# Small weights loaded half by half between x's tile pairs, and multiplied with the first pair before the second pair is transposed

## The chip, the core and the metric

The kernel runs on one core of a Trainium2 chip. The metric is the device time of one execution in microseconds (us). The core has five engines that run side by side, each through its own instructions in order: TensorE (PE in the profile, its weight loads PEld), VectorE (DVE), ScalarE (ACT), GpSimd (POOL) and SyncE (SP), which here only issues DMA transfers. Matrix products land in PSUM, and everything else is kept in SBUF.

## The reference, cut to what matters

One encoder layer over 512 tokens of width 1024: an RMS norm, one wide input projection, sparse attention over keys that an indexer picks (group A), latent attention (group B), gates, and one output projection with a residual. The change lies wholly in the first lines: the norm, and the two narrow columns of the projection.

```python
xn = rms_norm(h, norm_gain[l])          # (512, 1024)
proj = xn @ w_in[l]                     # (1024, D_IN)
(q_a, k_a, v_a, g_a, q_i, k_i, w_i,
 c_q, c_kv, k_rope, g_b) = jnp.split(proj, offsets, axis=-1)
...
k_i = jnp.concatenate([rope(k_i[..., :IDX_ROPE_DIM], pos), k_i[..., IDX_ROPE_DIM:]], axis=-1)
o_a = indexer_sparse_attention(q_a, k_a, v_a, q_i, k_i, w_i, pos)
```

The "small weights" are 104 of w_in's columns: 32 for `k_rope`, and 72 for `k_i` and `w_i`. `q_i` is the first wide projection (512 columns).

## The kernel before, in words

Every matrix product is made of three, because each operand is kept as a high part (rounded to the type that TensorE reads) and a low part (what the rounding left): high times high, high times low, low times high. `mm3` (L180) issues these three. So every operand costs two steps before TensorE can use it: a copy or scaling that makes the high part, nearly always on ACT, and a subtraction that makes the low part, on DVE or POOL.

The start of the program runs as follows. The token dimension is cut in four tiles of 128 (t = 0 to 3), and tiles 0 and 1 are the first pair (`xin` 0, half 0), tiles 2 and 3 the second (`xin` 1, half 1). Per tile: a DMA loads it (L198). ACT sums the squares of its first 512 columns and DVE those of the other 512 (L343, L344), DVE adds the two sums (L345), POOL raises the sum to the power -0.5 (`rsqrt`, L216), and DVE scales the tile with that (L350), in one instruction of 1024 columns, for tile 3 in two of 512. Then TensorE transposes the tile in eight pieces of 128 columns (`x_turn`, L130) into PSUM, eight k-pieces per pair. When both tiles of a pair are there, ACT makes `xh` from PSUM (L370) and DVE makes `xl` (L373), 16 instructions each over the whole start.

The small weights `smw` come by four DMAs (two halves of four k-pieces, each in a transfer of 32 and one of 72 columns), ACT casts each half to `swh` (L204), and POOL subtracts for `swl` (L205). `small_step(hf, k)` multiplies k-piece k of one pair (half hf of the tokens) with them: 3 products of 256 columns into the bank `sm_acc`.

The wide weights come in chunks of one k-piece: a DMA into `wst` (three buffers, L263), a cast on ACT to `wh` (L267), a subtraction to `wl` (L270) on POOL, for every fourth chunk of `q_i` on DVE. A DMA into a `wst` buffer waits until the subtraction that reads the buffer's former chunk is done. So the subtractions set the pace of the loads.

TensorE's order is the order of the code. Before: the transposes of all four tiles, then `small_step(0, 0..7)`, then `small_step(1, k)` in turns with steps of `q_i` for tiles 1 to 3. The order on the other engines comes from a scheduler that works on an estimate of times, within the order that `after` (L221) forces by hand.

Later, `use_small` transposes the small result on TensorE, ACT copies it to `sm` (L431), and a row of DVE instructions (L438 to L442, then L410, L413 and L509 for the first tile of `q_i`) leads to the transposes of that tile (`turn` in `use_qi`), which TensorE has in its order among the wide products.

Of the kernel before, what the change touches and what calls it, by code (L numbers as in the profile page):

```python
# [16 lines left out]
D = 1024  # L17
# [67 lines left out]
def layer(ctx: ExitStack, tc: tile.TileContext, x, norm_gain, w_in, a_q_norm, a_k_norm, b_q_latent,  # L85
# [11 lines left out]
    def sb(tag, shape, dt=F32, name=None):  # L97
        return P.tile(list(shape), dt, name=name or tag, tag=tag, bufs=BUFS[tag])
# [8 lines left out]
    def psum(tag):  # L107
        return PS.tile([128, 512], F32, name=tag, tag=tag, bufs=BANKS[tag])

    def f32(ap):  # L110
        return ap.bitcast(F32)
# [39 lines left out]
    def run(g):  # L151
        for _ in g:
            tick()

    def take(g, n):
        for _ in range(n):
            if next(g, None) is None:
                return
            yield 1
# [34 lines left out]
    wst = sb("qk8", (128, 8, 104), name="smw")  # L194
    wv = w_in.rearrange("(k p) c -> p k c", p=128)
    SWH, SWL = sb("V", (128, 8, 104), F32R, "swh"), sb("V", (128, 8, 104), F32R, "swl")
    for t in range(NT):
        nc.sync.dma_start(xin[t // 2][:, t % 2], xv[:, t])  # L198
        if t == NT - 1:
            for a in range(0, 8, 4):  # L200
                ks = slice(a, a + 4)
                nc.sync.dma_start(wst[:, ks, 0:32], wv[:, ks, 3272:3304])
                nc.sync.dma_start(wst[:, ks, 32:104], wv[:, ks, 2560:2632])
                nc.scalar.copy(SWH[:, ks], wst[:, ks])  # L204
                nc.gpsimd.tensor_tensor(SWL[:, ks], wst[:, ks], f32(SWH[:, ks]), op=OP.subtract)  # L205
        if t == 1:
            nc.sync.dma_start(ident, cst[:, 768:896])
            nc.sync.dma_start(grow[0:8], norm_gain.rearrange("(k p) -> k p", p=128))
            nc.sync.dma_start(grow[8:11], b_q_latent.rearrange("(k p) -> k p", p=128))
            nc.sync.dma_start(grow[11:13], b_kv_latent.rearrange("(k p) -> k p", p=128))  # L210

    nhalf = P.tile([128, 8], F32, name="nhalf")
    nc.gpsimd.memset(nhalf, -0.5)
# [97 lines left out]
    def stream(jobs, group=2, banks=("mm",), skew=True):  # L311

        order, start = [], 0
        for i, (nk, _, _) in enumerate(jobs):
            s = start if skew else start - start % nk
            order += [(s + k, i, k) for k in range(nk)]
            start += nk / group
        acc = {}
        for _, i, k in sorted(order):
            nk, step, use = jobs[i]  # L320
            if k == 0:
                acc[i] = psum(banks[i % len(banks)])
            step(acc[i], k)
            if k == nk - 1:
                use(acc.pop(i))
            yield 1
# [12 lines left out]
    for t in range(NT):  # L339
        xt = xin[t // 2][:, t % 2]  # L340
        r = small(4)
        sq = tmp(), tmp()
        nc.scalar.activation(sq[0], xt[:, 0:512], AF.Square, scale=D ** -0.5, accum_out=r[:, 0:1])  # L343
        nc.vector.tensor_tensor_reduce(sq[1], xt[:, 512:], xt[:, 512:], 1.0 / D, EPS, OP.mult, OP.add, r[:, 1:2])  # L344
        nc.vector.tensor_tensor(r[:, 2:3], r[:, 0:1], r[:, 1:2], op=OP.add)  # L345
        rsqrt(r[:, 3:4], r[:, 2:3])
        w = D // 2 if t == NT - 1 else D
        for a in range(0, D, w):
            xs = xt[:, a:a + w]
            nc.vector.tensor_scalar(xs, xs, r[:, 3:4], None, op0=OP.mult)  # L350
    gp = psum("pv")
    transpose(gp[:, :13], grow[:13], ident[:13, :13])
    nc.scalar.copy(gains, gp[:, :13])


    xb = {}

    def x_turn(t):
        hf = t // 2
        if t % 2 == 0:  # L360
            xb[hf] = [psum(b) for b in (("tr", "tr", "sc", "sc"), ("mm", "mm", "mm", "tr"))[hf]]
        for k in range(8):
            c = (k % 2) * 256 + (t % 2) * 128
            transpose(xb[hf][k // 2][:, c:c + 128], xin[hf][:, t % 2, k * 128:k * 128 + 128], ident)
        parts = lambda k: [xb[hf][k // 2][:, (k % 2) * 256:(k % 2) * 256 + 256]] + [
            f(k)[:, hf * 256:hf * 256 + 256] for f in (xh, xl)]
        for b in range(0, 8 if t % 2 else 0, 2):
            for k in (b, b + 1):
                p, h, l = parts(k)
                nc.scalar.activation(h, p, AF.Copy, scale=gains[:, k:k + 1])  # L370
            for k in (b, b + 1):
                p, h, l = parts(k)
                nc.vector.scalar_tensor_tensor(l, p, gains[:, k:k + 1], f32(h), op0=OP.mult, op1=OP.subtract)  # L373
# [98 lines left out]
    def lat_kv(_, a):  # L472
        latent(a, 11, ckv, ckvs, "pt2")

    for t in range(NT):
        x_turn(t)
    sm_acc = psum("pv")

    def small_step(hf, k):
        c = slice(hf * 256, hf * 256 + 256)  # L480
        mm3(sm_acc[:104, c], SWH[:, k], SWL[:, k], xh(k)[:, c], xl(k)[:, c], k == 0, k == 7)

    for k in range(8):
        small_step(0, k)
    qi_ = stream(tok_jobs("q_i", 8, xh, xl, 512, [1, 2, 3], lambda t, a: use_qi(t, a)), 3, skew=True)
    for k in range(8):
        small_step(1, k)
        run(take(qi_, 1))
        if k == 2:
            nc.sync.dma_start(cs32, cst[:, 512:768])  # L490
    nc.sync.dma_start(wide, cst[:, 896:1408])
# [474 lines left out]
```

## Time and profile before

| | us |
|---|---|
| median of 3 runs | 347.33 (346.73 to 347.7) |
| the profiled execution | 345.63 |
| its span in the trace | 343.8 |
| around the span (345.63 - 343.8) | 1.83 |
| TensorE busy | 326.7 (95% of the span) |
| DVE busy | 265.5 (77%) |
| ACT busy | 219.6 (64%) |
| POOL busy | 182.2 (53%) |

The trace is one execution; engines are rows of instructions with a start and a duration. Where an instruction found its engine idle, a bracket says how long the engine sat idle and whose work ended the wait. Start-up is the time in which TensorE is not yet busy without breaks, here the first 13.3 us. TensorE's granted clock is at its full 2.4 GHz throughout.

### The profile page before, as it was taken

How to read it: one execution, taken by the hardware profiler on the slowest of the kernel's cores; microseconds unless marked ns; L12 is line 12 of the kernel's file. 1: busy time of each engine (PE TensorE's matmuls, PEld its weight loads, DVE VectorE, ACT ScalarE, POOL GpSimd, SP SyncE). 2: the span in 40 equal slices, each digit the busy share in tenths (PEclk: the TensorE clock that was granted, in tenths of full speed). 3: DMA queues.
4: the chain of work that ended last, by engine and by line, in shares of the span. 5: the costliest groups of instructions: out<-in, count | busy, mean ns of one | idle time of the engine just before them, and what ended most of it. 6: DMA issues, size and time to landing. Idle time of an engine off the chain costs nothing.

```text
span 343.8 us, 5465 instructions
## 1 busy us (share of the span) xinstructions
PE 326.7 (95%) x1688; PEld 271.9 (79%) x1688; DVE 265.5 (77%) x634; ACT 219.6 (64%) x536; POOL 182.2 (53%) x193
## 2 busy tenths in 40 slices
PE   2999899999899999999999999999999999999995
PEld 2887787888688788788888788888888788788884
DVE  4925787759999797877779987679898776877466
ACT  4934558574757776878876898434526988878210
POOL 1745462166697998315623469519924635457100
PEclk9999999999999999999999999999999999999999
DMA  7753344124032433103320055515697324410006
GB/s 267 196 151 98 84 132 126 29 94 122 2 99 71 113 92 102 54 2 92 92 64 0 1 128 159 144 24 141 170 212 216 126 79 137 120 66 0 2 0 244
DMA packets 28806, 34.83 MB, mean 101 GB/s; under 512 B 5341, under 2 KB 16874, under 8 KB 28778
## 3 DMA queue, kind: packets, MB, share of 16 engines
q1 hardware_dynamic: 28202, 33.57, 34.7%
q10 hardware_dynamic: 576, 0.92, 0.7%
q8 instruction: 13, 0.21, 0.3%
q14 instruction: 15, 0.12, 0.1%
HBM read 27.14 MB, written 2.10 MB: 85 GB/s over the span
## 4 chain that ended last, share of the span: by engine, by line
PE 49%; DVE 17%; POOL 11%; DMA 8%; issue 6%; ACT 6%; SPq 1%; POOLq 0%; DVEq 0%; ACTq 0%
PE mm L126 28%; PE sc L126 7%; DMA wst<-in_w_in 7%; PE pv L126 6%; PE tr L130 5%; POOL wl L270 4%; POOL sml L216 4%; DVE acc L555 2%; DVE ob L923 2%; DVE m L554 2%; PE mm L130 2%; DVE z L694 2%; ACT wh L267 2%; ACT z L696 1%; DVE wl L270 1%
## 5 line engine op out<-in xcount | busy, mean ns | idle before, releaser
L270 POOL TENSOR_TENSOR wl<-wst,wh 128x512 fp32r<-128x512 f32 (+2 forms) x79 | 98.3, 1253 | 59.3 <-ACT wh L267 47.9
L267 ACT CAST wh<-wst 128x512 fp32r<-128x512 f32 (+2 forms) x89 | 50.9, 586 | 30.2 <-DMA wst<-in_w_in 22.0
L126 PE MATMUL mm<-wh,xh 128*128 128x512 f32 x120 | 50.2, 419 | 0.0
L126 PE MATMUL mm<-wl,xh 128*128 128x512 f32 x120 | 47.6, 397 | 0.2 <-POOL wl L270 0.2
L126 PE MATMUL mm<-wh,xl 128*128 128x512 f32 x120 | 47.4, 395 | 0.0
L216 POOL TENSOR_TENSOR sml<-sml,nhalf 128x4 f32<-128x4 f32 (+2 forms) x28 | 32.0, 1149 | 25.9 <-ACT sml L825 14.8
L696 ACT ACTIVATE z<-z,sml 128x256 f32<-128x256 f32 (+2 forms) x64 | 35.9, 561 | 11.1 <-DVE sml L694 10.0
L713 POOL TENSOR_SCALAR z<-z,sml 128x512 f32<-128x512 f32 (+2 forms) x32 | 18.2, 570 | 41.6 <-DVE sml L709 31.4
L126 PE MATMUL mm<-xh,wh 128*128 128x512 f32 x80 | 33.3, 417 | 0.0
L126 PE MATMUL mm<-xl,wh 128*128 128x512 f32 x80 | 31.7, 396 | 0.0
L126 PE MATMUL mm<-xh,wl 128*128 128x512 f32 x80 | 31.6, 395 | 0.0
L126 PEld LDWEIGHTS mm<-wh,xl 128*128 128x128 f32 x120 | 22.6, 188 | 5.3
L554 DVE MAX8 m<-acc 128x8 f32<-128x512 f32 (+2 forms) x48 | 26.3, 549 | 0.0
L555 DVE MATCH_REPLACE8 acc<-m,acc 128x512 f32<-128x512 f32 (+2 forms) x48 | 25.9, 540 | 0.0
L126 PEld LDWEIGHTS mm<-wl,xh 128*128 128x128 f32 x120 | 22.8, 190 | 3.5 <-POOL wl L270 0.5
L126 PEld LDWEIGHTS mm<-wh,xh 128*128 128x128 f32 x120 | 22.7, 189 | 3.0
L694 DVE CUSTOM_DVE_ANT_0 z<-sc,wide,nqb 128x512 f32<-128x512 f32 (+3 forms) x32 | 17.4, 543 | 6.4 <-PE sc L126 6.2
L416 DVE TENSOR_TENSOR pl<-tr,ph 128x512 fp32r<-128x512 f32 (+1 forms) x32 | 17.6, 551 | 5.9 <-ACT ph L416 5.6
L416 ACT CAST ph<-tr 128x512 fp32r<-128x512 f32 (+1 forms) x32 | 15.2, 474 | 8.0 <-PE tr L130 7.6
L126 PE MATMUL sc<-kl,bhl 96*128 96x512 f32 (+3 forms) x96 | 20.2, 322 | 0.0
L126 PEld LDWEIGHTS sc<-kl,bhl 96*128 96x128 f32 x96 | 16.6, 189 | 3.2 <-DVE bhl L794 0.3
L923 DVE TENSOR_TENSOR ob<-mm,ob 128x512 f32<-128x512 f32 (+1 forms) x25 | 16.5, 667 | 2.9 <-PE mm L126 2.6
(214 smaller groups left out, 884.6 us busy)
## 6 DMA issues: line engine op xcount, KB each, us to landing
wst<-in_w_in SPq DMA_DIRECT2D x48, 256.0 KB, 2.7
wst<-in_w_out SPq DMA_DIRECT2D x16, 256.0 KB, 2.9
xin<-in_x SPq DMA_DIRECT2D x4, 512.0 KB, 4.1
k_a<-tmp SPq DMA_DIRECT2D x16, 128.0 KB, 3.5
ob<-in_x SPq DMA_DIRECT2D x8, 256.0 KB, 4.5
wst<-in_w_in SPq DMA_DIRECT2D x8, 192.0 KB, 2.6
wst<-in_w_uq SPq DMA_DIRECT2D x6, 192.0 KB, 2.3
wst<-in_w_in SPq DMA_DIRECT2D x8, 128.0 KB, 2.1
```

The costliest lines, as they stand in the source:

```text
L126: nc.tensor.matmul(o, l, r, start=start, stop=stop)
L130: nc.tensor.transpose(o, i, idn)
L216: nc.gpsimd.tensor_tensor(dst, src, nhalf[:, :src.shape[-1]], op=OP.pow)
L267: copies.append(nc.scalar.copy(h, st))
L270: i = E(eng).tensor_tensor(l, st, f32(h), op=OP.subtract)
L416: return nc.scalar.copy(h, p), nc.vector.tensor_tensor(l, p, f32(h), op=OP.subtract)
L554: nc.vector.max(m, masks[t])
L555: dve[0] = nc.vector.match_replace(masks[t], m, masks[t], -3e38).ins
L694: m = nc.vector.tensor_tensor_reduce(z, sc[:, :n], mask(t), nq(h, t), 3e38, OP.add, OP.min, r[:, i:i + 1])
L696: e = nc.scalar.activation(z, z, AF.Exp, bias=r[:, i:i + 1], scale=-1.0, accum_out=r[:, 2 + i:3 + i])
L713: nc.gpsimd.tensor_scalar(z, z, w, 0.0, op0=OP.mult, op1=OP.add)
L923: nc.vector.tensor_tensor(o, p[:, :n], o, op=OP.add)
```

## The change

The four small constant loads (`ident` and three gains) go from SP's DMA queue to ACT's, ahead of ACT's work. On SP's queue the first half of the small weights comes after tiles 0 and 1 and the second half after tiles 2 and 3. TensorE transposes tiles 0 and 1, does `small_step(0, 0..3)`, transposes tiles 2 and 3, and goes on with `small_step(0, 4..7)`. The second half of tile 3 is scaled on ACT instead of DVE. Three orders are forced by hand: the sum of squares of tile 3 on ACT behind the `xh` of the first pair's k-piece 3, the cast of the second half of the small weights behind the scaling of tile 3's second half, and the casts of the first three `q_i` chunks behind the cast of the small weights and each behind two more `xh`.

```diff
+    nc.scalar.dma_start(ident, cst[:, 768:896])
+    nc.scalar.dma_start(grow[0:8], norm_gain.rearrange("(k p) -> k p", p=128))
+    nc.scalar.dma_start(grow[8:11], b_q_latent.rearrange("(k p) -> k p", p=128))
+    nc.scalar.dma_start(grow[11:13], b_kv_latent.rearrange("(k p) -> k p", p=128))
     for t in range(NT):
         nc.sync.dma_start(xin[t // 2][:, t % 2], xv[:, t])
-        if t == NT - 1:
-            for a in range(0, 8, 4):
-                ks = slice(a, a + 4)
-                nc.sync.dma_start(wst[:, ks, 0:32], wv[:, ks, 3272:3304])
-                nc.sync.dma_start(wst[:, ks, 32:104], wv[:, ks, 2560:2632])
-                nc.scalar.copy(SWH[:, ks], wst[:, ks])
-                nc.gpsimd.tensor_tensor(SWL[:, ks], wst[:, ks], f32(SWH[:, ks]), op=OP.subtract)
-        if t == 1:
-            nc.sync.dma_start(ident, cst[:, 768:896])
...
+        if t % 2:
+            ks = slice(t // 2 * 4, t // 2 * 4 + 4)
+            nc.sync.dma_start(wst[:, ks, 0:32], wv[:, ks, 3272:3304])
+            nc.sync.dma_start(wst[:, ks, 32:104], wv[:, ks, 2560:2632])
+            swc = nc.scalar.copy(SWH[:, ks], wst[:, ks])
+            nc.gpsimd.tensor_tensor(SWL[:, ks], wst[:, ks], f32(SWH[:, ks]), op=OP.subtract)
...
             xs = xt[:, a:a + w]
-            nc.vector.tensor_scalar(xs, xs, r[:, 3:4], None, op0=OP.mult)
+            if a:
+                xsc = nc.scalar.activation(xs, xs, AF.Copy, scale=r[:, 3:4])
+            else:
+                nc.vector.tensor_scalar(xs, xs, r[:, 3:4], None, op0=OP.mult)
...
-                nc.scalar.activation(h, p, AF.Copy, scale=gains[:, k:k + 1])
+                e = nc.scalar.activation(h, p, AF.Copy, scale=gains[:, k:k + 1])
+                xev[hf, k] = e
+                if (hf, k) == (0, 3):
+                    after(sqa, e)
...
-    for t in range(NT):
-        x_turn(t)
-    sm_acc = psum("pv")
...
+    x_turn(0)
+    x_turn(1)
+    sm_acc = psum("pv")
     for k in range(8):
+        if k == 4:
+            x_turn(2)
+            x_turn(3)
         small_step(0, k)
+    after(swc, xsc)
     qi_ = stream(tok_jobs("q_i", 8, xh, xl, 512, [1, 2, 3], lambda t, a: use_qi(t, a)), 3, skew=True)
     for k in range(8):
         small_step(1, k)
         run(take(qi_, 1))
+        if k == 0:
+            for i, c in enumerate(copies[:3]):
+                after(c, swc)
+                after(c, xev[1, 2 * i + 1])
```

TensorE, start of the program, as a difference (`xin_63` is the first pair, `xin_64` the second; `pv<-xh,swh` and its like are the small products, of which a third use `xl` and a third `swl`):

```order
 L130 MATMUL tr<-ident,xin_63 128x128 x4
 L130 MATMUL sc<-ident,xin_63 128x128 x4
-L130 MATMUL mm<-ident,xin_64 128x128 x6
-L130 MATMUL tr<-ident,xin_64 128x128 x2
-L130 MATMUL mm<-ident,xin_64 128x128 x6
-L130 MATMUL tr<-ident,xin_64 128x128 x2
 L126 MATMUL pv<-xh_89,swh 104x256
 L126 MATMUL pv<-xl_91,swh 104x256
```

The 16 transposes of the second pair now stand behind the first 12 small products, and the other 12 small products behind those transposes.

DVE from the second tile's scaling to the last scaling, before (`ISA` with `xin` is the sum of squares, `ISA sml` its read-out, `TENSOR_SCALAR` the scaling, `SCALAR_TENSOR_TENSOR` makes `xl`):

```order
L344 ISA tmp,sml<-xin_64 128x512
L344 ISA sml 128x1
L350 TENSOR_SCALAR xin_63<-xin_63,sml 128x1024
L345 TENSOR_TENSOR sml<-sml 128x1
L344 ISA tmp,sml<-xin_64 128x512
L344 ISA sml 128x1
L350 TENSOR_SCALAR xin_64<-xin_64,sml 128x1024
L345 TENSOR_TENSOR sml<-sml 128x1
L373 SCALAR_TENSOR_TENSOR xl_91<-tr,gains,xh_89 128x256 x2
L350 TENSOR_SCALAR xin_64<-xin_64,sml 128x512 x2
L373 SCALAR_TENSOR_TENSOR xl_91<-tr,gains,xh_89 128x256 x2
```

The same place on DVE now:

```order
L352 TENSOR_SCALAR xin_63<-xin_63,sml 128x1024
L343 ISA tmp,sml<-xin_64 128x512
L343 ISA sml 128x1
L344 TENSOR_TENSOR sml<-sml 128x1
L352 TENSOR_SCALAR xin_64<-xin_64,sml 128x1024
L343 ISA tmp,sml<-xin_64 128x512
L343 ISA sml 128x1
L378 SCALAR_TENSOR_TENSOR xl_91<-tr,gains,xh_89 128x256 x4
L344 TENSOR_TENSOR sml<-sml 128x1
L378 SCALAR_TENSOR_TENSOR xl_92<-sc,gains,xh_90 128x256 x4
L352 TENSOR_SCALAR xin_64<-xin_64,sml 128x512
```

Each tile's scaling now stands directly behind that tile's sum, and the last scaling stands behind all eight `xl` of the first pair instead of behind two.

POOL at the same place now (`sml<-sml,nhalf` is the power -0.5 of one tile; before, all four stood in a row, and both `swl` behind them):

```order
L215 ISA
L215 TENSOR_TENSOR sml<-sml,nhalf 128x1 x2
L209 TENSOR_TENSOR swl<-smw,swh 128x416
L215 TENSOR_TENSOR sml<-sml,nhalf 128x1 x2
L209 TENSOR_TENSOR swl<-smw,swh 128x416
L269 TENSOR_TENSOR wl<-wst,wh 128x512 x6
```

The first `swl` has moved between the powers of tiles 1 and 2.

ACT from the sum of squares of tile 2 on, now (`xh` of the second pair is written from `mm` and the last `tr`, `wh` are the chunks of `q_i`; before, the first `wh` stood ahead of the second pair's first `xh`):

```order
L342 ACTIVATE tmp,sml<-xin_64 128x512
L372 ACTIVATE xh_89<-tr,gains 128x256 x4
L342 ACTIVATE tmp,sml<-xin_64 128x512
L372 ACTIVATE xh_90<-sc,gains 128x256 x4
L350 ACTIVATE xin_64<-xin_64,sml 128x512
L208 CAST swh<-smw 128x416
L372 ACTIVATE xh_89<-mm,gains 128x256 x2
L266 CAST wh<-wst 128x512
L372 ACTIVATE xh_89<-mm,gains 128x256 x2
L266 CAST wh<-wst 128x512
```

The first two `wh` now each stand behind two `xh` of the second pair. Behind this place the rows of all engines are the same as before, but for the `wst` buffers: chunk 5 of `q_i` now takes the buffer that chunk 2 leaves, where before it took that of chunk 3.

## Rows read from the trace of the kernel before

**Rows 1.** Stretches: us, busy (x instructions) of PE, PEld, DVE, ACT, POOL; clock, DMA.

```profile
0.00:13.33 13.33, 6.17 (x33) 5.44 (x34) 8.08 (x21) 8.03 (x21) 3.90 (x11) 1.00 0.90 285
13.33:34.13 20.80, 20.59 (x115) 17.06 (x113) 10.34 (x24) 11.04 (x26) 12.39 (x12) 1.00 0.41 109
```

**Rows 2.** TensorE's waits, whole program: who waited for whom, us, times, longest.

```profile
PE sc L126 <- DVE vb L642: 2.0, 3, 1.4
PE tr L130 <- DVE tmp L509: 0.9, 1, 0.9
PE tr L126 <- DVE acc L546: 0.8, 1, 0.8
...
PE tr L130 <- DVE kil L416: 0.3, 1, 0.3
```

**Rows 3.** Timeline, TensorE: start, duration, operation, count, [idle before, releaser].

```profile
12.94 0.44 PE L130 MATMUL mm<-ident,xin 128*128 128x128 f32 x2 [0.55 <-DVE xin L350]
...
13.35 0.36 PE L126 MATMUL pv<-xh,swh 128*104 128x256 f32 x1
...
16.61 0.40 PE L126 MATMUL mm<-wh,xh 128*128 128x512 f32 x1
...
19.32 0.50 PE L126 MATMUL mm<-wl,xh 128*128 128x512 f32 x1 [0.21 <-POOL wl L270]
...
27.97 0.52 PE L130 MATMUL tr<-ident,tmp 104*128 104x104 f32 x4
...
35.07 0.63 PE L130 MATMUL tr<-ident,tmp 128*128 128x128 f32 x4 [0.94 <-DVE tmp L509]
```

**Rows 4.** Timeline, DVE, start-up.

```profile
7.13 0.69 DVE L344 CUSTOM_DVE_ANT_0 tmp<-xin 128x512 f32<-128x512 f32 x1 [0.26 <-DMA xin<-in_x]
...
7.75 0.75 DVE L350 TENSOR_SCALAR xin<-xin,sml 128x1024 f32<-128x1024 f32 x1
8.41 0.15 DVE L345 TENSOR_TENSOR sml<-sml 128x1 f32<-128x1 f32 x1
...
11.20 1.68 DVE L350 TENSOR_SCALAR xin<-xin,sml 128x512 f32<-128x512 f32 x2
...
13.60 1.64 DVE L373 SCALAR_TENSOR_TENSOR xl<-sc,gains,xh 128x256 fp32r<-128x256 f32 x4
```

**Rows 5.** Timeline, POOL, start-up.

```profile
6.95 0.56 POOL L216 TENSOR_TENSOR sml<-sml,nhalf 128x1 f32<-128x1 f32 x1 [1.19 <-DVE sml L345]
...
11.24 1.36 POOL L205 TENSOR_TENSOR swl<-smw,swh 128x416 fp32r<-128x416 f32 x1 [0.34 <-ACT swh L204]
13.51 1.09 POOL L205 TENSOR_TENSOR swl<-smw,swh 128x416 fp32r<-128x416 f32 x1 [0.90 <-ACT swh L204]
```

**Rows 6.** Timelines: DVE's second half of tile 3's scaling alone, from a narrower window.

```profile
11.60 1.29 DVE L350 TENSOR_SCALAR xin<-xin,sml 128x512 f32<-128x512 f32 x1
```

**Rows 7.** Timelines of DVE and POOL: three subtractions of the wide weights.

```profile
19.33 0.69 DVE L270 TENSOR_TENSOR wl<-wst,wh 128x512 fp32r<-128x512 f32 x1 [0.91 <-ACT wh L267]
...
25.86 1.30 POOL L270 TENSOR_TENSOR wl<-wst,wh 128x512 fp32r<-128x512 f32 x1 [1.14 <-ACT wh L267]
...
26.44 1.26 DVE L270 TENSOR_TENSOR wl<-wst,wh 128x512 fp32r<-128x512 f32 x1 [6.42 <-ACT wh L267]
```

**Rows 8.** Timeline, ACT.

```profile
9.55 1.19 ACT L370 ACTIVATE xh<-tr,gains 128x256 fp32r<-128x256 f32 x3
10.62 0.54 ACT L204 CAST swh<-smw 128x416 fp32r<-128x416 f32 x1
...
13.27 0.67 ACT L267 CAST wh<-wst 128x512 fp32r<-128x512 f32 x1
...
30.22 0.50 ACT L431 COPY sm<-tr 128x416 f32<-128x416 f32 x1
```

**Rows 9.** Timeline, SP: start and duration of the first two issues.

```profile
0.73 0.86 SPq L198 DMA_DIRECT2D xin<-in_x  x2
```

**Rows 10.** DMA issues to 30 us: KB each, median us from issue to landing.

```profile
smw<-in_w_in SPq DMA_DIRECT2D x2, 144.0 KB, 4.5
```

More of the change, by code (lines that the diff above doesn't have):

```diff
@@ L196, in layer @@
     SWH, SWL = sb("V", (128, 8, 104), F32R, "swh"), sb("V", (128, 8, 104), F32R, "swl")
+    nc.scalar.dma_start(ident, cst[:, 768:896])
+    nc.scalar.dma_start(grow[0:8], norm_gain.rearrange("(k p) -> k p", p=128))
+    nc.scalar.dma_start(grow[8:11], b_q_latent.rearrange("(k p) -> k p", p=128))
+    nc.scalar.dma_start(grow[11:13], b_kv_latent.rearrange("(k p) -> k p", p=128))
     for t in range(NT):
         nc.sync.dma_start(xin[t // 2][:, t % 2], xv[:, t])
-        if t == NT - 1:
-            for a in range(0, 8, 4):
-                ks = slice(a, a + 4)
-                nc.sync.dma_start(wst[:, ks, 0:32], wv[:, ks, 3272:3304])
-                nc.sync.dma_start(wst[:, ks, 32:104], wv[:, ks, 2560:2632])
-                nc.scalar.copy(SWH[:, ks], wst[:, ks])
-                nc.gpsimd.tensor_tensor(SWL[:, ks], wst[:, ks], f32(SWH[:, ks]), op=OP.subtract)
-        if t == 1:
-            nc.sync.dma_start(ident, cst[:, 768:896])
-            nc.sync.dma_start(grow[0:8], norm_gain.rearrange("(k p) -> k p", p=128))
-            nc.sync.dma_start(grow[8:11], b_q_latent.rearrange("(k p) -> k p", p=128))
-            nc.sync.dma_start(grow[11:13], b_kv_latent.rearrange("(k p) -> k p", p=128))
+        if t % 2:
[4 more added lines that the diff above has]
+            nc.gpsimd.tensor_tensor(SWL[:, ks], wst[:, ks], f32(SWH[:, ks]), op=OP.subtract)
     nhalf = P.tile([128, 8], F32, name="nhalf")
@@ L342, in layer @@
         sq = tmp(), tmp()
-        nc.scalar.activation(sq[0], xt[:, 0:512], AF.Square, scale=D ** -0.5, accum_out=r[:, 0:1])
+        sqa = nc.scalar.activation(sq[0], xt[:, 0:512], AF.Square, scale=D ** -0.5, accum_out=r[:, 0:1])
         nc.vector.tensor_tensor_reduce(sq[1], xt[:, 512:], xt[:, 512:], 1.0 / D, EPS, OP.mult, OP.add, r[:, 1:2])
@@ L353, in layer @@
     nc.scalar.copy(gains, gp[:, :13])
-    xb = {}
+    xb, xev = {}, {}
     def x_turn(t):
```

## The prediction

> **What bounds the kernel now.** I read the share of busy time first: TensorE is at 95% of the span, so the time is its work plus its idle time. The table of stretches says where that idle time is: of the first 13.33 us TensorE works 6.17, so 7.16 us are idle, and in the next 20.80 us it works 20.59 [rows 1]. From then on its largest waits are 2.0, 0.9, 0.8 and 0.3 us, all for DVE [rows 2]. So start-up is the one place with something to win, and a shift of TensorE there goes through to the end, unless one of those later waits takes it up.
>
> Then I read who sets start-up. DVE's rows from 7.13 to 13.60 stand end to end [rows 4]: it does one job after the other for four tiles, and TensorE's transposes of the last piece wait 0.55 us for a scaling on DVE [rows 3]. The small products then run from 13.35 without a break, and the first product of `q_i` starts at 16.61 [rows 3]. The only wait behind it up to 34.13 (35.07 less the 0.94 us of idle time before it) is at 19.32, for the third `wl` from POOL [rows 3]. So the order of work on DVE decides when the second pair is transposed, and POOL's subtractions decide when `q_i` gets going. Both are touched.
>
> **The change part by part.**
>
> What it aims at is easy to price: 12 of the small products (27 stand between 13.35 and 16.61, so 0.12 us each, 1.45 us in all [rows 3]) go into idle time. That is worth up to 1.45 us if the second pair is transposed as early as before. It is not, by the following walk, and DVE is its first half.
>
> Step 1, tile 1's scaling. POOL ends the power for tile 1 at 6.95 + 0.56 = 7.51 [rows 5]. Before, POOL then had nothing to do but the next power; now the first `swl` is next. Is its input there? SP is free behind two issues at 0.73 + 0.86 = 1.59 [rows 9], the second small transfer is issued about 0.4 later, at 2.0, lands 4.5 later [rows 10], at 6.5, and the cast takes 0.54 [rows 8]: 7.05, so yes, with half a microsecond to spare. Then POOL goes from one instruction into the next at 7.51, while DVE's scaling of tile 1 must first hear of it. What happens when the two meet is in the trace: the second half of tile 3's scaling took 1.29 us [rows 6], where the pair of halves, less this, leaves some 0.48 for the first [rows 4], and it ended at 12.89, 0.29 behind the `swl` that ran on POOL from 11.24 to 12.60 [rows 5]. A subtraction of wide weights on DVE took 1.26 us beside one on POOL that ran until 27.16, and 0.69 alone [rows 7]. So a DVE instruction that reads SBUF in this way stands still until POOL's is through. Here `swl` lasts 1.09 [rows 5], to 8.60, and the scaling, of twice the columns, ends 2 x 0.29 behind it: 9.18. Without that it would end at 7.55 + 0.75 = 8.30.
>
> The Trainium skill has the rule for this ("SBUF — State Buffer", section "Who interferes with whom"): DVE and GpSimd share one pair of SBUF ports, which whoever comes first holds for its whole instruction. It speaks against putting `swl` between two scalings, and the trace agrees with the 1.29 us against 0.48. The page also counts DVE instructions with two SBUF inputs; by that the sum of squares would be held too, and a late `swl` would cost no less than an early one: the sum is the same.
>
> Step 2, tile 2. DVE's order now is sum, add, scaling with nothing between, where before it did the next tile's sum while POOL took the power. From 9.18: the sum starts 0.08 ahead of the end and lasts 0.70 with its read-out, the add 0.15 [rows 4], to 9.95; 0.08 later POOL's power, 0.56 [rows 5], to 10.59; the scaling 0.75 [rows 4], to 11.40. So 0.7 us of DVE's time go into waiting for POOL.
>
> Step 3, to the last scaling. Sum of tile 3 to 12.02; four `xl` (1.64 for four, 0.40 from start to start [rows 4]) to 13.62; the add to 13.72; four more `xl` to 15.32; then the half of tile 3's scaling that stays on DVE, 0.48: it ends at T = 15.80. Before, both halves were done at 12.89. The half that ACT takes saves DVE 0.4 to 0.5 us and is not late: the power of tile 3 ends some 0.65 behind the add, at 14.4, and ACT needs one 0.6 us instruction. I set it at nothing.
>
> Step 4, from T to `q_i`. Two transposes, 0.44 [rows 3], and 0.05 to get there: 16.29. Two `xh` at 0.36 each (1.19 for three, with overlap [rows 8]): 17.01. Only then the first `wh`, 0.67 [rows 8], since the change puts the casts behind two `xh` each: 17.68. POOL then needs 1.30 for each `wl` [rows 7], three of them with 0.05 in front: 21.63. So the product that started at 19.32 [rows 3] starts at about 21.68, 2.36 later. TensorE's own way is as long: eight transposes at 0.22 (1.76), 12 small products (1.45), three more (0.36), then two steps of about 1.05 and one product: 15.85 + 1.76 + 1.45 + 0.36 + 2.10 + 0.23 = 21.75. The later chunks each follow the subtraction that frees their buffer and have room at this pace.
>
> Step 5, what is given back. The 0.94 us wait at 35.07 [rows 3] ends a chain of DVE work that starts with ACT's copy of the small result at 30.22 [rows 8]. TensorE had its transposes ready at 27.97 + 0.52 = 28.49 [rows 3], 1.73 earlier. With TensorE 2.36 later they end at 30.85, so the chain moves by only 0.66, and ends at 35.73, while TensorE arrives at 34.13 + 2.36 = 36.49. The wait is gone, and 2.36 - 0.94 = 1.42 us remain. The later waits [rows 2] hang on DVE instructions that follow these transposes, so they move along and give nothing back.
>
> Step 6, the four constant loads on ACT's queue. They take SP's issue time off tiles 2 and 3 and put about as much (some 1.4 us) on ACT ahead of its first input, which is idle there. Nothing.
>
> Sum: 345.63 + 1.42 = 347.05 for the profiled execution. The median of the runs is 347.33, 1.70 above that execution, so in runs it is 348.75; I say 348.7 (+0.4%). A measurement can tell about 0.3%, here 1.04 us, from no change.
>
> **Bounds.** The lower end of T is DVE's work without the stop: scaling to 8.30, tile 2's scaling to 10.52, T = 14.92, which leaves 0.54 us. The upper end is a late transfer: past 8.3 each microsecond is one on T.
>
> **The rivals.**
>
> *The port is free* (0.18): `swl` falls beside nothing, or the meeting costs less on 1024 columns than on 512. T = 14.92, and +0.54: 347.9, within 0.3%. Against it stand the two meetings [rows 6, 7].
>
> *The small transfer is late* (0.10): it now runs behind two x tiles and ahead of two. If it lands at 9.5 instead of 6.5, the cast is done at 10.04, `swl` at 11.2, and the power for tile 2, which stands behind it on POOL, at 11.8 instead of 10.59: +1.2 on top, 349.9. Its landing took 4.5 us with x tiles ahead of it too [rows 10], which speaks against so long a delay.
>
> *The loss is given back later* (0.14): the 2.0, 0.8 and 0.3 us of later waits [rows 2] are for DVE; if DVE has room by then, TensorE's delay shrinks by about as much as these waits hold, to between 0 and 0.5: 347.3 to 347.8.
>
> *Faster* (0.08): the second pair is not delayed, and the 12 products do go into idle time. The place is the last half scaling on DVE, and the point is T = 15.80 - 1.42 = 14.38: before it the change gains. At the 12.89 of before it would gain 1.49: 345.8. For it speaks that TensorE idles for 7.16 us ahead of 13.33 [rows 1]; against it, that DVE's rows alone, with no stop by POOL, already add up to 14.92.
>
> That the products don't go ahead is no rival: the order has them there. They will wait for the `xl` of their piece, from 12.4 to 13.6.
>
> **How the numbers follow.** The main case has 0.50, the rivals 0.18, 0.10, 0.14 and 0.08. Within the main case T may be off by half a microsecond, and about a fifth of it falls under 1.04 us. Slower by over 0.3%: 0.40 + 0.10 = 0.50; within 0.3%: 0.10 + 0.18 + 0.14 = 0.42; faster: 0.08. The range leaves out the faster case and the outer ends of the others: from 347.2, just under the case where all is given back, to 350.0, the late transfer.
>
> **What the profile of the changed kernel would show.** Step 1: tile 1's scaling takes 1.3 to 1.7 us beside a POOL `swl`; 0.75 would be the free port. Step 2: DVE idle for 0.6 to 0.7 us ahead of tile 2's scaling. Step 3: the first transposes of the second pair's last tile start near 15.8. Step 4: the first `wh` near 17, the third `wl` done near 21.6, TensorE waiting for it or just not. Step 5: no wait ahead of the transposes at 35.07, which now start near 36.5. The forecast is wrong if those transposes start before 35.6, or if TensorE's idle time behind them is smaller than before by a microsecond.

## The result, and the profile after

| | before | changed |
|---|---|---|
| median of 20 runs, us | 345.92 (344.65 to 347.7) | 347.95 (346.76 to 350.14) |
| ratio, 95% interval | | 1.0057 (1.004 to 1.0074) |
| the profiled execution, us | 345.63 | 348.55 |
| its span, us | 343.8 | 346.7 |
| TensorE busy, us | 326.7 | 328.8 (95%) |

The change makes the kernel 0.6% slower, about 2 us. The forecast was 1.42 us.

First the stretches of the changed kernel (us, busy and instructions of PE, PEld, DVE, ACT, POOL; clock, DMA), which answer to [rows 1]:

```profile
0.00:13.33 13.33, 4.91 (x20) 4.11 (x21) 6.93 (x17) 7.07 (x18) 3.03 (x10) 1.00 0.89 284
13.33:34.13 20.80, 20.64 (x115) 17.64 (x114) 8.96 (x21) 11.97 (x27) 11.31 (x11) 1.00 0.36 96
```

TensorE worked 6.17 us ahead of 13.33 before and works 4.91 now: of the 12 small products that were to fill the idle time, only three start in it. TensorE's waits (who for whom, us, times, longest), which answer to [rows 2], say for what it waits:

```profile
PE sc L126 <- DVE vb L654: 2.0, 3, 1.4
PE pv L126 <- DVE xl L378: 1.1, 1, 1.1
...
PE sc L126 <- DVE bhl L806: 0.3, 1, 0.3
PE tr L130 <- DVE tmp L521: 0.3, 1, 0.3
```

The small products wait 1.1 us for the first `xl`. The wait ahead of the first turn of `q_i` (`tr` for `tmp`) fell from 0.9 to 0.3, so 0.65 was given back there. The 2.0 for `vb` is as before, and 0.3 for `bhl` is new. Now TensorE in order (start, duration, operation, [idle before, releaser]), which answers to [rows 3]:

```profile
11.16 0.56 PE L126 MATMUL pv<-xh,swh 128*104 128x256 f32 x1
12.82 0.54 PE L126 MATMUL pv<-xl,swh 128*104 128x256 f32 x1 [1.10 <-DVE xl L378]
13.16 0.41 PE L126 MATMUL pv<-xh,swl 128*104 128x256 f32 x1
13.37 0.41 PE L126 MATMUL pv<-xh,swh 128*104 128x256 f32 x1
...
15.29 1.38 PE L130 MATMUL mm<-ident,xin 128*128 128x128 f32 x6
...
16.73 0.82 PE L130 MATMUL mm<-ident,xin 128*128 128x128 f32 x6
...
19.37 0.39 PE L126 MATMUL mm<-wh,xh 128*128 128x512 f32 x1
...
22.41 0.50 PE L126 MATMUL mm<-wl,xh 128*128 128x512 f32 x1
...
31.07 0.52 PE L130 MATMUL tr<-ident,tmp 104*128 104x104 f32 x4
...
37.52 0.63 PE L130 MATMUL tr<-ident,tmp 128*128 128x128 f32 x4 [0.29 <-DVE tmp L521]
```

The small products start 0.21 apart (13.16, 13.37), where the 27 of before started 0.12 apart. They hold the transposes of tile 2 until 15.29, and those of tile 3 follow at 16.73. The first product of `q_i` moved from 16.61 to 19.37, the product with the third `wl` from 19.32 to 22.41 (+3.09), and the first turn of `q_i` from 35.07 to 37.52 (+2.45). Behind that, each row of TensorE stands 2.4 us later than before up to 139, and 2.9 from 142, behind the wait for `bhl`. Nothing is given back later.

The pace of 0.21 is that of TensorE's lower clock. Ahead of the prediction the granted clock was read as full throughout; that is wrong for start-up. The trace keeps the clock as stretches, each with a share, and the first of them, at 1.00 (the 2.4 GHz level), begins at 11.24 in the kernel before and at 16.44 in the changed one. For the time before that the trace holds no stretch, and a clock of 1.00 in the rows there only says that none is on record. In all 14 traces, waits aside, TensorE runs at the slow pace up to the start of that stretch (transposes and small products 0.21 apart) and at the fast one behind it (0.11 and 0.12): the transposes of tile 2 in the changed kernel are 0.21 apart up to 16.35 and 0.11 from 16.51. One trace has a stretch at 0.50, the 1.2 GHz level, within start-up, and TensorE runs 0.21 apart there too (turns_all_first, below). So, by its pace, the changed kernel ran at the lower level up to 16.44. Tile 2's transposes take 1.44 us there (15.29 to 16.73), tile 3's at full clock 0.79.

DVE and POOL at start-up, which answer to [rows 4, 5]:

```profile
7.93 1.55 DVE L352 TENSOR_SCALAR xin<-xin,sml 128x1024 f32<-128x1024 f32 x1 [0.67 <-POOL sml L215]
9.40 0.68 DVE L343 CUSTOM_DVE_ANT_0 tmp<-xin 128x512 f32<-128x512 f32 x1
...
11.01 0.75 DVE L352 TENSOR_SCALAR xin<-xin,sml 128x1024 f32<-128x1024 f32 x1 [0.65 <-POOL sml L215]
...
15.49 0.47 DVE L352 TENSOR_SCALAR xin<-xin,sml 128x512 f32<-128x512 f32 x1
```

```profile
7.87 1.06 POOL L209 TENSOR_TENSOR swl<-smw,swh 128x416 fp32r<-128x416 f32 x1
...
18.57 3.79 POOL L269 TENSOR_TENSOR wl<-wst,wh 128x512 fp32r<-128x512 f32 x3 [1.61 <-ACT wh L266]
```

Tile 1's scaling takes 1.55 beside the `swl`, and DVE waits 0.65 for the power of tile 2. The last scaling ends at 15.96. ACT and SP:

```profile
9.04 0.63 ACT L342 ACTIVATE tmp<-xin 128x512 f32<-128x512 f32 x1 [1.79 <-DMA xin<-in_x]
...
17.88 0.62 ACT L266 CAST wh<-wst 128x512 fp32r<-128x512 f32 x1
...
32.34 0.41 ACT L266 CAST wh<-wst 128x256 fp32r<-128x256 f32 x1 [2.06 <-PE mm L126]
32.65 0.50 ACT L436 COPY sm<-tr 128x416 f32<-128x416 f32 x1
```

```profile
4.58 0.82 SPq L203 DMA_DIRECT2D xin<-in_x  x2
```

Tile 2 is issued at 4.58 (before at 3.11) and its sum of squares starts at 9.04 (before at 7.13). The first `wh` moved from 13.27 to 17.88, and the copy to `sm`, with which the chain to the turn begins, from 30.22 to 32.65.

### The profile page after: what moved, and what is told of

The parts are those of the page before. It is cut to its first block, busy times and chain, and to the rows that moved or that the text cites. A ratio compares the mean times of both kernels' runs of the same rounds, so it can differ in the third digit from the quotient of the medians.

```text
span 346.7 us, 5464 instructions
## 1 busy us (share of the span) xinstructions
PE 328.8 (95%) x1688; PEld 273.3 (79%) x1688; DVE 265.3 (77%) x633; ACT 220.7 (64%) x537; POOL 181.8 (52%) x193
## 4 chain that ended last, share of the span: by engine, by line
PE 49%; DVE 20%; POOL 10%; DMA 7%; ACT 6%; issue 6%; SPq 1%; DVEq 0%; POOLq 0%; ACTq 0%
PE mm L126 28%; PE sc L126 7%; PE pv L126 6%; PE tr L130 4%; POOL sml L215 4%; POOL wl L269 4%; DMA wst<-in_w_in 4%; DVE acc L567 3%; DVE m L566 3%; DVE ob L935 2%; PE mm L130 2%; DVE z L706 2%; DMA xin<-in_x 2%; ACT z L708 1%; ACT wh L266 1%
```

## The experiments

All runs stand beside runs of the kernel before on the same chip. The place at which to read each is the first turn of `q_i`, since a shift there goes through to the end: the spans of the profiles differ from that of before by this shift and -0.2 to 0.8 us more, old_loads alone by 1.7 more. It has two inputs: TensorE's own way, and the copy to `sm` with the DVE chain behind it. In the six kernels in which TensorE waited there (before, the changed one, and four below), the turn came 4.85 to 4.89 behind that copy. The last column is the start of the clock's first stretch at 1.00 in the profile, 11.24 before. The turn is read from one execution of each kernel, and this clock is part of it; the ratio is from all runs.

| kernel | ratio to before (95%) | turn, against 35.07 | TensorE waited there | clock full from |
|---|---|---|---|---|
| changed | 1.0057 (1.004 to 1.0074) | +2.45 | 0.29 | 16.44 |
| turn2_first | 1.0067 (1.0046 to 1.0089) | +1.57 | no | 13.79 |
| turns_all_first | 1.0113 (1.0086 to 1.014) | +4.30 | no | 10.98, but for 14.39 to 21.22 |
| no_first_swl | 1.0052 (1.0033 to 1.0071) | +1.44 | no | 15.60 |
| consts_on_sp | 1.0074 (1.0058 to 1.009) | +1.73 | 0.48 | 11.47 |
| small_behind_x | 1.0041 (1.0024 to 1.0057) | +1.12 | 0.48 | 11.51 |
| old_loads | 1.0035 (1.0014 to 1.0056) | +0.79 | 0.65 | 10.31 |
| only_loads | 1.0116 (1.0092 to 1.014) | +3.08 | no | 19.64 |
| half_on_act | 0.998 (0.9964 to 0.9996) | -0.85 | no | 12.68 |
| orders_free | 1.0021 (1.0006 to 1.0037) | +0.18 | no | 10.55 |
| casts_free | 1.0086 (1.0063 to 1.011) | +3.04 | no | 16.22 |
| turn_order | 1.0021 (1.0007 to 1.0034) | +0.97 | no | 16.00 |
| half_first | 1.0004 (0.9991 to 1.0016) | +0.50 | 0.78 | 10.18 |

### TensorE's order, undone in part and in full

turn2_first, on the changed kernel: tile 2's transposes go back ahead of the small products.

```diff
     x_turn(1)
+    x_turn(2)
     sm_acc = psum("pv")
     for k in range(8):
         if k == 4:
-            x_turn(2)
             x_turn(3)
```

> The changed kernel, with tile 2's eight transposes back ahead of the first 12 small products; tile 3's stay behind them. Theory of the DVE chain (DVE's order and POOL's first swl make tile 3 late, and TensorE's order adds a part of its own): the last scaling on DVE still ends near 16.0, tile 3's transposes start there instead of at 16.73, the third chunk's wl product of q_i (22.41 in the changed kernel) comes 0.6 to 0.7 us earlier, the transposes of q_i's first tile (37.52) 0.3 to 0.7 earlier; runs about 1.5 us over the kernel before. Rival, TensorE's order alone makes the loss: tile 2's transposes cost nothing and nothing moves, or all 2 us come back. Rival, TensorE's order doesn't matter: no row moves by more than 0.2.

347.71 us. turns_all_first moves `x_turn(3)` up too, which is TensorE's order of before:

> The changed kernel, with all 32 transposes ahead of all small products on TensorE, as before the change; loads, POOL's and DVE's order stay changed. Theory of the DVE chain: the last scaling on DVE still ends near 16.0, tile 3's transposes end near 17.1, 24 small products stand behind them, q_i starts near 20.1 (19.37 in the changed kernel): no better than the changed kernel, 0 to 0.7 us worse in the trace. Rival, the moved products make the loss: q_i starts near 16.6 as in the kernel before and the runs are back at its time.

349.77 us, more than was expected; `q_i` starts at 22.49 in it. TensorE waits 2.31 us for tile 3, and its profile is the one whose clock row falls in start-up (stretches, columns as above):

```profile
14.00:15.00 1.00, 0.00 (x0) 0.00 (x0) 1.00 (x3) 0.38 (x1) 0.55 (x1) 0.70 0.20 41
15.00:16.00 1.00, 0.02 (x1) 0.02 (x1) 0.92 (x3) 0.77 (x2) 0.15 (x1) 0.50 0.24 54
16.00:19.00 3.00, 3.00 (x14) 3.00 (x15) 1.05 (x3) 2.30 (x6) 1.79 (x2) 0.50 0.03 7
```

The granted clock is 0.50, the level of 1.2 GHz, from 14.39 to 21.22; it fell while TensorE did nothing (13.67 to 15.98), and the small products there start 0.21 apart. With the change's loads, then, the order with small products ahead is 1.9 us better (349.77 - 347.88, taking the changed kernel at 1.0057 of that series' 345.91): it is not what loses. But not all of this is idle time filled. Two of the four executions (350.08, the profiled one, and 350.17) have a mean clock of 0.99, to which such a fall brings it; the others (348.72 and 349.46, at 1.00) lie 0.8 and 1.6 over 347.88. Moving tile 2 alone brings the turn 0.88 forward in the profile, and the runs show no gain.

### The stop on DVE

no_first_swl leaves out part of the computation: the low part of the first half of the small weights is set to zero, so no POOL subtraction runs between the powers.

```diff
+    nc.gpsimd.memset(f32(SWL[:, 0:4]), 0.0)
...
+            if t == 3:
-            nc.gpsimd.tensor_tensor(SWL[:, ks], wst[:, ks], f32(SWH[:, ks]), op=OP.subtract)
+                nc.gpsimd.tensor_tensor(SWL[:, ks], wst[:, ks], f32(SWH[:, ks]), op=OP.subtract)
```

> The changed kernel without POOL's subtraction for the low part of the first half of the small weights (it is zeroed at the start instead, so that part of the small products is left out). Theory of the lock as one part among several: the scaling of tile 1 takes 0.75 us instead of 1.55, but the sum of tile 2 can't start before that tile lands at 9.04, so the last scaling on DVE comes only 0.3 to 0.4 us earlier, and the q_i rows and the runs 0.2 to 0.4. Rival, the lock is the main cause: 0.9 us or more come back, and the runs are within 1 us of the kernel before. Rival, the lock costs nothing: the scaling still takes over 1.3 us.

347.68 us, not to be told from the changed kernel. DVE's rows:

```profile
7.79 0.75 DVE L354 TENSOR_SCALAR xin<-xin,sml 128x1024 f32<-128x1024 f32 x1 [0.67 <-POOL sml L217]
...
9.11 0.69 DVE L345 CUSTOM_DVE_ANT_0 tmp<-xin 128x512 f32<-128x512 f32 x1 [0.56 <-DMA xin<-in_x]
...
15.22 0.48 DVE L354 TENSOR_SCALAR xin<-xin,sml 128x512 f32<-128x512 f32 x1
```

The scaling takes 0.75 instead of 1.55, so the stop is real. But DVE then waits 0.56 for tile 2, and the last scaling ends at 15.70 instead of 15.96 (T, as in the prediction). The stop hid behind a late transfer; of its 0.8 us only 0.26 reached T.

### The loads

consts_on_sp puts the four constants back on SP's queue behind tile 1 and holds DVE's order.

```diff
-    nc.scalar.dma_start(ident, cst[:, 768:896])
...
+        if t == 1:
+            nc.sync.dma_start(ident, cst[:, 768:896])
...
+        if t >= 2:
+            after(sqv, scl)
```

> The changed kernel with the four constant loads back on SP's queue behind tiles 0 and 1, with DVE's order held as in the changed kernel. Theory that the loads on ACT's queue delay x: tile 0 is used at 4.07 instead of 4.38, tile 1 at 5.44 instead of 5.83, tile 2's sum on ACT starts by 8.3 instead of 9.04, DVE's whole chain moves 0.3 to 0.5 us earlier and the q_i rows with it; runs 0.3 to 0.5 us under the changed kernel. Rival, the forecast's view that these loads cost nothing: the first sums start at 4.38 and 5.83 as now, nothing moves.

348.11 us. Tiles 0 and 1 come 0.2 and 0.3 earlier than in the changed kernel (sums of squares at 4.19 and 5.49), but that of tile 2 starts at 9.11, no earlier. The turn stands 0.72 earlier in this profile, whose clock was full from 11.47; the runs show no gain. small_behind_x moves both halves of the small weights behind tile 3:

```diff
-        if t % 2:
+        if t == NT - 1:
+            for a in range(0, 8, 4):
+                ks = slice(a, a + 4)
```

> The changed kernel, but both halves of the small weights are loaded behind tile 3, so that no small transfer stands between the pairs; the constants stay on ACT's queue, TensorE's order, the half scaling on ACT and the three forced orders stay. DVE's order comes out as in before up to tile 2 (sum of tile 2 ahead of tile 1's scaling). Theory 1, the second pair comes late (tile 2 landed at 9.04 instead of 7.13): tile 2 lands at 7.2 to 7.8, the last scaling ends at T = 14.0 to 14.8 instead of 15.96, and the first turn of q_i moves from 37.52 to 36.0 to 36.6: 346.4 to 347.0. Theory 2, the loss lies in the new order of TensorE and of the casts, not in the loads: T falls as much, but the third wl of q_i still comes at 22 or later, because the small weights now come later and the casts hang on them, and the time stays within 0.5 of the changed kernel, 347.5 to 348.3. In either case the 12 small products ahead wait for the first swl, which needs the cast of a transfer that now comes last.

347.69 us. old_loads does both:

> As small_behind_x, with the constants back on SP's queue between the pairs too, so that all loads stand as in before, and only TensorE's order, the half scaling on ACT and the forced orders of the change are left. Theory 1: tiles 0 and 1 begin 0.3 to 0.4 us earlier, tile 2 lands at 7.1 to 7.5, T is 0.2 to 0.4 below that of small_behind_x: 346.0 to 346.7, at most 0.8 above before. Theory 2: still 347.3 to 348.0.

347.58 us. The sums of squares of tile 2 in these two:

```profile
8.06 0.69 DVE L344 CUSTOM_DVE_ANT_0 tmp<-xin 128x512 f32<-128x512 f32 x1 [0.89 <-DMA xin<-in_x]
```

```profile
6.94 0.69 DVE L345 CUSTOM_DVE_ANT_0 tmp<-xin 128x512 f32<-128x512 f32 x1
```

The tile needs both moves to be back (9.04, then 8.06, then 6.94). T falls to 14.96 and 14.37 and the turn to 36.19 and 35.86, near what theory 1 has; but the times miss it, with ratios of 1.0041 and 1.0035 against 1.0057, and the intervals of all three overlap. In both the turn waits for the copy to `sm` (0.48, 0.65), which comes at 31.33 and 30.97, since the first `wh` is still as late as the forced order makes it (16.18, 15.80, before 13.27). old_loads loses a further 1.4 us behind the turn: its waits for `vb` are 3.4 in 4 places instead of 2.0 in 3.

```profile
PE sc L126 <- DVE vb L656: 3.4, 4, 1.4
```

only_loads is the counterpart, the kernel before with the change's loads and nothing else.

> The other side: the kernel before with the change's loads alone (constants on ACT's queue, the halves of the small weights between and behind the pairs). TensorE's order, the scaling on DVE and the order of the casts are those of before. Theory 1: tile 2 lands at 8.8 to 9.2, tile 3's scaling ends 2 to 3 us later than the 12.89 of before, and the time is 347.2 to 348.3, nearly the whole loss or more, since no small product fills the wait. Theory 2: 345.9 to 346.6.

350.21 us, 4.04 more than before: theory 1's sign, and far more than the changed kernel loses. Four of its six executions (349.80 to 351.36) have a mean clock of 0.99, as after the fall in turns_all_first, so part of the 4.04 is likely the clock, though none of the four has a trace that shows where it fell; the two at 1.00 (348.72, the profiled one, and 349.67) lose 2.6 and 3.5. Tile 3's two halves are scaled from 14.17 to 15.86, again beside the second `swl` (POOL, 14.45 to 15.57), and all 24 small products stand behind that:

```profile
14.17 1.69 DVE L349 TENSOR_SCALAR xin<-xin,sml 128x512 f32<-128x512 f32 x2
```

So the loads by themselves lose, and the rest of the change wins part of it back; with it the mean clock is 0.997 or more in all 20 executions. That they are what loses in the changed kernel is not shown to the same degree: old_loads takes them back and gains no more than the noise.

### The forced orders

orders_free is the changed kernel without its three forced orders (its four `after` lines taken out).

> The changed kernel without its three forced orders; loads, TensorE's order and the half scaling on ACT stay. The sum of squares of tile 3 then comes behind two xh instead of four, DVE scales its half of tile 3 behind six xl instead of eight, and the q_i casts stand ahead of the second pair's xh. Theory 1, TensorE's own way to the first turn of q_i decides (37.23 without the wait, in the changed kernel), and it hangs on T: T moves from 15.96 to 14.7 to 15.3, the turn to 36.0 to 36.6: 346.6 to 347.2. Theory 2, the late tile 2 alone decides and the forced orders only fill in behind it: T stays at 15.7 or later and the time within 0.4 of the changed kernel.

347.01 us, ratio 1.0021, and the intervals of the two (1.0006 to 1.0037, 1.004 to 1.0074) don't meet: the forced orders cost about 1.2 us. T on ACT ends no earlier (16.01), so it is not T: the first `wh` starts at 14.20 instead of 17.88, SP issues the next chunks from 17.13 instead of 19.89, and the copy to `sm` comes at 30.47 instead of 32.65. TensorE arrives at the turn at 35.25 without a wait (ACT, then TensorE):

```profile
14.20 1.19 ACT L266 CAST wh<-wst 128x512 fp32r<-128x512 f32 x2
...
30.47 0.50 ACT L436 COPY sm<-tr 128x416 f32<-128x416 f32 x1
```

```profile
35.25 0.60 PE L130 MATMUL tr<-ident,tmp 128*128 128x128 f32 x4
```

Theory 1's time holds, but not through T. The profile leaves one doubt: its clock was full from 10.55 instead of 16.44, so the small products run 0.12 apart, which brings tile 2's transposes to 14.13 instead of 15.29. The 1.2 us of the runs are the three orders' together; how much is the casts' alone is not settled.

casts_free frees only the casts.

```diff
             for i, c in enumerate(copies[:3]):
-                after(c, swc)
-                after(c, xev[1, 2 * i + 1])
+                pass
```

> The changed kernel without one of the three forced orders: the first three q_i casts no longer stand behind the second pair's xh. ACT then makes all three ahead of the half scaling, some 1.7 us, so this half ends at 16.3 or later instead of 15.3, but the wl are done 3 us earlier and the buffers of the wide weights come free earlier. If the casts and so the loads set the turn of q_i, it moves from 37.52 to 36.5 or less: 346.9 or less. If TensorE's own way does, the later half makes it slightly worse: 347.9 to 348.5.

349.09 us, worse than either case. The casts do come earlier, but POOL then has all three `wl` ahead of the second `swl`, and TensorE's small products wait for it (POOL, then TensorE):

```profile
14.58 3.94 POOL L269 TENSOR_TENSOR wl<-wst,wh 128x512 fp32r<-128x512 f32 x3
18.48 1.06 POOL L209 TENSOR_TENSOR swl<-smw,swh 128x416 fp32r<-128x416 f32 x1
```

```profile
19.60 0.37 PE L126 MATMUL pv<-xh,swl 128*104 128x256 f32 x1 [1.71 <-POOL swl L209]
```

I had counted what the casts hold back on ACT and not who stands next on POOL.

### The kernel before with one part of the change

half_on_act scales the second half of tile 3 on ACT, and changes nothing else.

```diff
-            nc.vector.tensor_scalar(xs, xs, r[:, 3:4], None, op0=OP.mult)
+            if a:
+                nc.scalar.activation(xs, xs, AF.Copy, scale=r[:, 3:4])
+            else:
+                nc.vector.tensor_scalar(xs, xs, r[:, 3:4], None, op0=OP.mult)
```

> The kernel before with one edit: the second half of tile 3 is scaled on ACT instead of DVE. In before this half took 1.29 us on DVE beside the swl on POOL. If that stop sets T there, T falls from 12.89 to 12.2 to 12.5, TensorE's wait of 0.55 ahead of the last transposes goes, and the time falls by 0.3 to 0.5: 345.4 to 345.6. If ACT is late instead (its xh stand in front), T stays at 12.9 and the time within 0.2 of before. A loss would come from the xh of the first pair, moved by 0.7 us on ACT.

345.47 us, ratio 0.998 (0.9964 to 0.9996): faster than both kernels, though only just clear of no change against the kernel before, by somewhat more than expected, and not in the way expected. TensorE waits longer for the last pieces, and still the turn comes 0.85 earlier:

```profile
13.67 0.44 PE L130 MATMUL mm<-ident,xin 128*128 128x128 f32 x2 [0.71 <-ACT xin L351]
...
34.22 0.60 PE L130 MATMUL tr<-ident,tmp 128*128 128x128 f32 x4
```

In [rows 3] these stand at 12.94 and 35.07, the second with a wait of 0.94. TensorE arrives at 34.22, as before (34.13); what went is the wait. ACT takes the three casts at 13.89, 15.14 and 16.37, POOL makes the three `wl` without a gap from 15.17 to 18.98 (before, the third ended at 19.26), and the copy to `sm` comes at 29.11 instead of 30.22.

half_first forces that half ahead of the first pair's last four `xh` on ACT:

```diff
+                if hf == 0 and k >= 4:
+                    after(e, xsc)
```

> half_on_act with the half scaling on ACT forced ahead of the four xh of the first pair's last pieces. In half_on_act that half ended at 13.54 behind them, and TensorE waited 0.71 for it. Now it ends near 12.1, ahead of DVE's tail; TensorE's last transposes start near 12.3, the first product of q_i near 16.4 instead of 17.34. Where TensorE's own way sets the turn of q_i (34.22, no wait), it gains what the third wl leaves: 0.3 to 0.8, 344.7 to 345.2. Where the chain behind the copy to sm is as late, 345.3 to 345.5, no gain.

346.25 us, no different from before. `q_i` starts at 16.90, earlier than in half_on_act (17.34), and the gain is lost: the scheduler puts six `xh` between the second and the third cast instead of two, so the third comes at 17.83 instead of 16.37, and the copy to `sm` at 30.71 instead of 29.11:

```profile
17.83 0.73 ACT L267 CAST wh<-wst 128x512 fp32r<-128x512 f32 x1
```

```profile
35.57 0.63 PE L130 MATMUL tr<-ident,tmp 128*128 128x128 f32 x4 [0.78 <-DVE tmp L514]
```

turn_order is half_on_act with TensorE's order of the change.

```diff
+    x_turn(0)
+    x_turn(1)
...
+        if k == 4:
+            x_turn(2)
+            x_turn(3)
         small_step(0, k)
```

> half_on_act (345.47, 0.998 of before) with TensorE's order of the change, and nothing else: 12 small products ahead of the second pair's transposes; loads and all other orders as in before. It differs from old_loads (347.58) only by the three forced orders, and from half_on_act only by TensorE's order. The second pair is scaled by 13.5 here, and the small products wait for the first swl at 12.6, so the last transposes start near 14.8 instead of 13.67. If TensorE's order loses, 346.3 to 347.0; if the forced orders are what old_loads loses, within 0.4 of half_on_act, 345.2 to 345.9.

347.17 us: TensorE's order loses 0.4% where the loads are those of before (the intervals of the two don't meet). The second pair is scaled by 13.99 there; but the small products ahead of its transposes wait 0.98 for the cast and 0.69 for `swl`, then run 0.21 apart (the clock was full only from 16.00), and the transposes of tile 2 start at 15.29, as in the changed kernel:

```profile
11.59 0.54 PE L126 MATMUL pv<-xh,swh 128*104 128x256 f32 x1 [0.98 <-ACT swh L204]
...
13.03 0.54 PE L126 MATMUL pv<-xh,swl 128*104 128x256 f32 x1 [0.69 <-POOL swl L205]
```

The parts need each other, then. Small products ahead need early small weights; early small weights make the second pair late. With either alone the kernel loses 1.4 us (turn_order against half_on_act, by the ratios) or 4.0 us (only_loads, at the lower mean clock); with both, 2.0.

## Why the prediction was right, and where it was off

The sign and the size of the main case held: 348.7 was forecast and 347.95 measured, with the kernel before at 345.92 in these runs instead of the 347.33 from which the forecast counted; 1.42 us were forecast and about 2.0 measured (0.57% of 345.92, 0.40 to 0.74%). So the time came out closer than the loss: the three runs that it counted from lay 1.4 us above the median of 20.

Step 1, tile 1's scaling, held. It was forecast at 1.3 to 1.7 us beside the `swl` and took 1.55, to 9.48 (forecast 9.18; it began at 7.93 instead of 7.55). The rule of the Trainium skill ("SBUF — State Buffer", section "Who interferes with whom"), that of DVE and GpSimd the first at the shared SBUF ports holds them for its whole instruction, is borne out on 1024 columns: 1.55 beside POOL's 1.06, and 0.75 in no_first_swl. What it is worth was wrong: the lower bound, T = 14.92 without the stop, counted DVE's work alone and took tile 2 as there. It came at 9.04, and no_first_swl gave T = 15.70. By these, the rival of the free port, +0.54, was no possible outcome of this change. The sign stood in the trace of the kernel before: DVE's rows from 7.13 on don't quite stand end to end, as the prediction has it, but wait 0.26 us for tile 2 [rows 4] and, at 8.84, 0.28 for tile 3.

Step 2 held: DVE waits 0.65 for the power, and tile 2's scaling starts at 11.01 (forecast 10.65). Step 3 held in its number: T = 15.96, forecast 15.80. That is in part luck, since the late tile 2 alone gives 15.70 and the stop, to which the prediction gave 0.88, adds 0.26.

Step 4 was too small: 2.36 forecast for the product with the third `wl`, 3.09 measured. The first `wh` came at 17.88, forecast near 17.0. The term that failed is the small products at 0.12 each, 1.45 for 12: the second of them waits until 12.82 and the 12th is followed by the transposes at 15.29, 2.47 us for 11, at the lower clock. So tile 2's transposes, for which the sum had room, were pushed onto the path, and tile 3's started at 16.73 instead of 15.85 to 16.0. The same step took tile 3's eight transposes at 0.22 each, 1.76, the pace of the lower clock; at full clock they took 0.79. The two errors cancel, and `q_i` starts at 19.37, where the step's terms give 19.42: luck. From there to the product with the third `wl` it is 3.04 instead of 2.33, since that `wl` was done at 22.36 (forecast 21.63), and POOL had begun with a first `wh` that was 0.9 late.

Step 5 was off, 0.94 forecast and 0.65 given back. The step took the small transposes as the start of the chain to the turn, and had the copy to `sm` move by 0.66, to 30.88. It moved by 2.43, to 32.65. ACT has the cast of a chunk of wide weights directly ahead of that copy, in the changed kernel from 32.34, in the kernel before from 29.91. The bracket of that cast names TensorE, but its load landed at 32.24, 0.10 ahead of it, and in the kernel before it stands 0.10 behind its load as well (29.81, 29.91). So the chain hangs on the loads of `q_i`, and these on the first three `wl`. The prediction's own row had shown the copy at 30.22 with the transposes done 1.73 us earlier; that gap should have been followed back.

Step 6, the constants at nothing, was wrong in the trace and right in the time. Tiles 0 and 1 come 0.3 to 0.4 later, and SP's issue of tile 2 stands at 4.58 instead of 3.11, because it waits 1.9 us for the transfer of `ident`. consts_on_sp shows no gain without them, since with the half of the small weights ahead of it tile 2 is as late (the last section tells why).

Taken together: TensorE's arrival at the turn moved by 3.10 (34.13 to 37.23) instead of 2.36, and 0.65 came back instead of 0.94, so 2.45 instead of 1.42. The rival of a late small transfer did not occur (`swl` started right behind the power, at 7.87); it was the x tile behind the transfer that came late. The loss is not given back later: the 2.0 for `vb` is unchanged.

The prediction's account of where the loss arises was incomplete. It put it on DVE, by T. The runs put it in three places that meet at the turn: tile 2's late load, the small products ahead, which in the profiled execution ran at the lower clock, and the forced orders (about 1.2 us), which hold the casts and with them the loads of `q_i`. Only the share of the forced orders is shown by runs; what the other two hold of the remaining 0.8 us is open.

## What to carry to other kernels

Where an operation is moved into idle time, ask what it needs there, and what is pushed back so that its input is early: here the weights that feed the filling work delayed the tile that everybody waits for. A wait late in the kernel is priced by following its chain back through the instruction that stands ahead in the engine's order, not through the data alone: the copy to `sm` waited for a cast of other weights. A profile of start-up also holds the clock of its one execution, so what a part is worth is read from the runs. Moving half an instruction to an engine with room (half_on_act) did better than the whole rearrangement, but not by the room itself: half_first moves the same half, has it done earlier, and gains nothing, since the third cast comes late again.

## What the runs showed of the hardware

TensorE ran small products of 256 columns at two paces, 0.12 and 0.21 us apart, and the pace goes with the granted clock: 0.21 up to the first stretch at 1.00 in each trace and in the stretch at 0.50 in turns_all_first, 0.12 elsewhere. A mean of the clock, as the rows give it, shows 1.00 also where the trace has nothing on record, so at the start of a program it is the pace that tells.

When the clock rose, the kernel's order does not settle. Up to 10.4 TensorE's rows are nearly alike in the changed kernel, casts_free, orders_free and turns_all_first (the first transposes start at 7.25, 7.23, 7.21 and 7.20, those of tile 1 at 9.54, 9.51, 9.50 and 9.49), and yet the clock was full from 16.44, 16.22, 10.55 and 10.98. What decides is open, since each kernel has one profile; runs of one kernel lie up to 3.6 us apart. In the profiled execution of the changed kernel the late rise costs about 0.7 us on the path: tile 3's transposes could have started when T allowed, near 16.0, as in orders_free (16.06), and started at 16.73.

A DMA issue can wait for another transfer that has nothing to do with its data: SP's issue of tile 2 waited 1.9 us for `ident`, which went over ACT's queue:

```profile
SPq L203 <- DMA ident<-cst: 1.9, 1, 1.9
```

The rows of all 14 traces show which one: the ninth transfer that the program issues, counted over both queues in the order of the code, starts when the first has landed. In the kernel before, the first is tile 0 (landed at 4.05) and the ninth a transfer of small weights (issued at 4.07), while tile 2 is the seventh. In the changed kernel `ident` is the first (landed at 4.56) and tile 2 the ninth (4.58). In consts_on_sp tile 2 is the ninth again and waits for tile 0 (4.16, 4.18). So four constants or two small transfers put ahead of a tile can cost it a wait, by their number and not by their size. Whether the chip or the program sets this count no run here shows.

With the constants on ACT's queue the x tiles came later although they were issued no later: in small_behind_x all four tiles were issued by 2.6 and landed at 4.29, 5.72, 8.04 and 9.42; in old_loads, with the constants between the pairs on SP's queue, tiles 2 and 3 were issued from 3.11, and the four landed at 4.05, 5.44, 6.92 and 8.94. What the transfers share was not tried.
